# Linear attention on one Trainium2 core: Q's features stored as pairs of rows and transposed as 4-byte elements, and half a block of V's masks moved from VectorE to ScalarE

## The chip, the cores and the metric

The kernel runs on 1 core of one Trainium2 chip. The metric is the device time of one execution in microseconds (us), smaller being better. Its engines are named as in the profile: PE (TensorE's matmuls), PEld (its weight loads), DVE (VectorE), ACT (ScalarE), POOL (GpSimd) and SP (SyncE). POOL and SP also issue DMA transfers, and the core's 16 DMA engines carry them.

## What is computed

Q, K and V are float32 of shape 8 x 12 x 512 x 64: 96 heads of 512 rows with 64 features. For each head:

```
Q_feat = max(0, Q) + 1
K_feat = max(0, K) + 1
KV = K_feat^T V                      (64 x 64)
K_sum = sum of K_feat over the rows  (64)
out = (Q_feat KV) / (Q_feat . K_sum + 1e-10)
```

There is no softmax and nothing of size 512 x 512. Every input is read once and every output written once: 37.75 MB read from HBM and 12.58 MB written.

## The kernel before

**Layout.** The rows of all heads form one long list. 4096 rows (8 heads, "an eight") lie in SBUF as 128 partitions of 32 consecutive rows, so a head occupies 16 partitions. Two eights form a stage, and there are 6 stages (s = 0 to 5). Each stage is worked as two groups, g = 2s and 2s + 1 (12 groups). For K and V a group is half of the stage's rows; for Q it is half of the 8 rows `c` of each of 4 runs `r` in a partition, for both eights `n`.

**Loads and stores.** `load_pair(s)` (L129) has POOL issue three transfers for a stage, V, K and Q in this order, each turning float32 into bfloat16 on the way (2 MB read, 1 MB written). Only stage 0 is cut into smaller loads; its first half of Q comes as float32 through SP. Raw inputs have two buffers each (`IN_BUFS`), so the loads of stage s + 2 wait until the raw tiles of stage s are used up. The loop at L359 issues `load_pair(s + 2)` behind iteration s. Stores of groups 0 to 5 are issued by POOL only behind the last load, one store per group (L363); groups 6 to 9 follow by POOL, and the last two groups are stored by SP in several pieces (L142 to L151).

**The work on a group.** DVE makes K's features (`k_features`, L158) and Q's (`q_features`, L175) by one instruction of two scalar operations for each eight. For the matmul that forms KV, V must be laid out so that four heads can share one accumulation: `v_blocks` (L165) writes V four times, block `b` multiplied by a column of ones and zeros (`mask[:, b]`) that keeps only the partitions of head `b`. DVE writes blocks 0 and 1 and the first half (eight n = 0) of block 2; ACT writes the other half of block 2 and block 3. `keys_values` (L182) runs 64 matmuls for a group on these; ACT copies the finished KV of a stage out of PSUM (`keys_values_copies`, L203). A column of V's layout holds the mask itself, so K_sum comes out as a 65th column.

Q must be turned so that its 64 features lie on partitions. `transposes` (L214) runs 16 TensorE transposes of 128 x 128 bfloat16 for a group: for each run `r` and each row `c` of the group's four, the two eights' 64 features side by side become 128 partitions. They fill two PSUM tiles `qt_ps` of 8 transposes each, and `transpose_copies` (L224) has ACT copy each tile (1024 elements per partition) into `qt`. There are two such PSUM tiles in all, so the next 8 transposes wait for ACT. `out_matmuls` (L229) then multiplies: 8 matmuls for each of a group's four PSUM cells, with 64 columns of `qt` as weights. `norms` (L246) has DVE take reciprocals of the denominators and multiply, which gives the output rows.

**Order.** The instructions are written out in order for each engine (`tc.manual_schedule`, `iteration`, L275). In iteration s, output of stage s - 1 is woven into the work on stage s. DVE's order is: norms of the first group of stage s - 1, the four Q features of stage s, K features and V blocks of its second group, norms of the second group of stage s - 1, then K features and V blocks of the next stage's first group. ACT's is: V blocks, four copies of `qt_ps`, V blocks, four copies of KV. In the last iteration (`end`), the K features and V blocks come first and the transposes of the second group come later.

The functions that the diff touches and their callers, with the profile's line numbers:

Of the kernel before, what the change touches and what calls it, by code (L numbers as in the profile page):

```python
# [8 lines left out]
FP32 = mybir.dt.float32  # L9
BF16 = mybir.dt.bfloat16  # L10
# [9 lines left out]
def kernel(  # L20
# [15 lines left out]
    nc = tc.nc  # L36

    B, H, S, D = Q.shape
    P = 128
    C = 8  # L40
    C2 = 2 * C
    C4 = 4 * C
    R = 4
# [15 lines left out]
    const = ctx.enter_context(tc.tile_pool(name="const", bufs=1))  # L59
    in_pool = ctx.enter_context(tc.tile_pool(name="in_pool", bufs=IN_BUFS))  # L60
    kf_pool = ctx.enter_context(tc.tile_pool(name="kf_pool", bufs=2))
    qf_pool = ctx.enter_context(tc.tile_pool(name="qf_pool", bufs=3))
    mid_pool = ctx.enter_context(tc.tile_pool(name="mid", bufs=2))
# [3 lines left out]
    psum = ctx.enter_context(tc.tile_pool(name="psum", bufs=2, space=bass.MemoryType.PSUM))  # L67
    psum_qt = ctx.enter_context(tc.tile_pool(name="psum_qt", bufs=2, space=bass.MemoryType.PSUM))

    identity = const.tile([P, P], BF16, name="identity")  # L70
    NV = 4
    v_all = const.tile([P, 2, 2, C2, 4, DV], BF16, name="v_all")

    mask_row = const.tile([P, 396], FP32, name="mask")
    mask = mask_row[:, 0:4]
    kva_all = const.tile([P, NV, 4, 2, D1], BF16, name="kva_all")
    kva_diag = [kva_all[:, i] for i in range(NV)]
# [5 lines left out]
    qfs = {}  # L83
    qts = {}
    outs = {}
    cells_of = {}
    qt_ps = {}
# [65 lines left out]
    def feature(dst, src):  # L153
        nc.vector.tensor_scalar(  # L154
            out=dst, in0=src, scalar1=1.0, scalar2=1.0, op0=ALU.add, op1=ALU.max
        )
# [8 lines left out]
    def v_blocks(g, engine):  # L165
        v_raw = raw["v", g]
        for b in range(4):
            block = v_all[:, g % 2, :, :, b, 0:D]
            cut = 2 if b < 2 else 1 if b == 2 else 0
            if engine == "dve" and cut > 0:  # L170
                nc.vector.tensor_scalar_mul(block[:, 0:cut], v_raw[:, 0:cut], mask[:, b : b + 1])  # L171
            if engine == "act" and cut < 2:
                nc.scalar.mul(out=block[:, cut:], in_=v_raw[:, cut:], mul=mask[:, b : b + 1])  # L173

    def q_features(g):  # L175
        q_raw = raw.pop(("q", g))
        qf = qf_pool.tile([P, R, C // 2, 2, D], BF16, name="qf")
        for n in range(2):
            feature(qf[:, :, :, n], q_raw[n])
        qfs[g] = qf  # L180

    def keys_values(g, lo=0, hi=C2):  # L182
# [29 lines left out]
                )  # L212

    def transposes(g):  # L214
        qf = qfs.pop(g)
        if g % 2 == 0:
            qts[g // 2] = mid_pool.tile([P, C, P, R], BF16, name="qt")
        qt_ps[g] = [psum_qt.tile([P, 2, R, P], BF16, name="qt_ps") for _ in range(2)]
        for half in range(2):
            for c in range(2):  # L220
                for r in range(R):
                    nc.tensor.transpose(qt_ps[g][half][:, c, r], qf[:, r, 2 * half + c, :, :], identity)  # L222

    def transpose_copies(g):  # L224
        for half, t in enumerate(qt_ps.pop(g)):
            lo = g % 2 * 4 + 2 * half
            nc.scalar.copy(out=qts[g // 2][:, lo : lo + 2], in_=t.rearrange("p c r q -> p c q r"))  # L227

    def out_matmuls(g, h, i):  # L229
        qt = qts[g // 2]  # L230
        kva = kva_diag[(g // 2 * 2 + h) % NV]
        o_ps = psum.tile([P, 2, BANK], FP32, tag="ps", name="o_ps")
        for c in range(4 * i, 4 * i + 4):
            for j in range(2):
                b = 2 * (g % 2) + j
                q = 16 * (4 * h + b)
                nc.tensor.matmul(  # L237
                    o_ps[64 * j : 64 * j + 64, c // 2 % 2, (c % 2) * W : (c % 2) * W + W],
                    lhsT=qt[:, c, q : q + 16, :],
                    rhs=kva[:, b],  # L240
                    start=True,
                    stop=True,
                )
        cells_of[g, h, i] = o_ps
# [18 lines left out]
    def output(g, between=()):  # L263

        cells = [(g, h, i) for h in range(2) for i in range(2)]
        for k in range(4):
            if k >= 2:
                norms(*cells[k - 2])
                if k - 2 < len(between):
                    between[k - 2]()  # L270
            out_matmuls(*cells[k])
        norms(*cells[2])
        norms(*cells[3])

    def iteration(s):  # L275
# [6 lines left out]
        def turned(g):  # L282
            transposes(g)
            transpose_copies(g)
# [12 lines left out]
        if end:  # L297
            k_features(b)
            v_blocks(b, "dve")
        v_blocks(b, "act")  # L300
        output(a - 2, [lambda lo=lo: keys_values(a, lo, lo + quarter) for lo in (0, quarter)])
        keys_values(a, 2 * quarter, C2)
        q_features(a)
        q_features(b)
        if not end:
            k_features(b)
            v_blocks(b, "dve")
# [14 lines left out]
    with tc.manual_schedule():  # L322
# [8 lines left out]
            out=mask,  # L331
            in_=identity.rearrange("p (h b x) -> p b h x", h=2, b=4),
# [3 lines left out]
        for i in range(2):  # L336
            t = v_all[:, i].rearrange("p n c b x -> p (n c) b x")
            nc.vector.memset(t[:, :, :, D1:], 0.0)
            nc.vector.tensor_copy(  # L339
                out=t[:, :, :, D], in_=mask[:, None, :].to_broadcast([P, 2 * C2, 4])  # L340
# [5 lines left out]
        blocks(0)  # L346
        keys_values(0)
        q_features(0)
        q_features(1)
        transposes(0)  # L350
        blocks(1)
        transpose_copies(0)
        transposes(1)
        transpose_copies(1)
        keys_values(1)
        load_pair(2)
# [42 lines left out]
```

## Time and profile before

| | |
|---|---|
| Time, median of 3 runs | 126.3 us (126.06 to 126.33) |
| The profiled execution: time, span of its instructions | 126.47 us, 124.7 us |
| PE busy / PEld busy | 72.2 us (58%) / 54.4 us (44%) |
| DVE busy | 81.9 us (66%), 185 instructions |
| ACT busy | 68.4 us (55%), 73 instructions |
| POOL busy | 24.8 us (20%) |
| Transposes, PE L222 | 192 of 219 ns, 13.7 us busy (they overlap) |
| Copies of `qt_ps`, ACT L227 | 24 of 1024 ns, 22.7 us |
| Q features, DVE L154 | 22 of 430 ns from bfloat16, 2 of 685 ns from float32 |
| V blocks on DVE, L171 | 24 of 759 ns (whole), 12 of 477 ns (half) |
| V blocks on ACT, L173 | 12 of 1998 ns (whole), 12 of 1158 ns (half) |
| HBM traffic over the span | 404 GB/s |

The profile is of one execution. The span runs from the first to the last instruction; the rest of the execution's time, 1.8 us here, lies around it. Busy time counts the time in which an engine ran at least one instruction, and its rows by slices or windows show when that was. The DMA share is the time that the 16 DMA engines' packets took, as a share of 16 times the stretch; overlapping packets can bring it a little above 1. GB/s counts bytes as they arrive, so a load that turns float32 into bfloat16 counts half of what it reads.

### The profile page before, as it was taken

The page shows a single profiled execution, that of the slowest core. Times are in us where ns is not written, and L with a number is a line of the kernel's source. Part 1 is how long each engine was busy: PE and PEld are TensorE (multiplying, and loading weights), DVE is VectorE, ACT ScalarE, POOL GpSimd, SP SyncE. Part 2 cuts the span into 40 slices and gives each one's busy share as a digit, 9 for nine tenths or more (in the row PEclk, how much of TensorE's full clock was granted, in tenths as well). Part 3 has the DMA queues.
Part 4 walks back from the last instruction along what each step waited for, and adds up shares of the span by engine and source line. Part 5 has one row for each costly group of instructions (what it writes and reads, how often), then busy time and mean ns, then how long its engine had stood idle before and what let it go on. Part 6 is the DMA issues. An engine that isn't in the chain of part 4 may idle for free.

```text
span 124.7 us, 3086 instructions
## 1 busy us (share of the span) xinstructions
PE 72.2 (58%) x1344; PEld 54.4 (44%) x1344; DVE 81.9 (66%) x185; ACT 68.4 (55%) x73; POOL 24.8 (20%) x52
## 2 busy tenths in 40 slices
PE   0000199692397949976796927979429995550000
PEld 0000299591266725754465714567216774320000
DVE  0475643006679997999979979798997945990000
ACT  0005827928955999199947998059990196000000
POOL 6990001500000600033000890220210202000000
PEclk9999999999859995899769995599975799955555
DMA  3999999999999999999999999999999999999991
GB/s 74 344 216 217 214 212 210 214 214 222 210 212 210 218 222 212 212 212 214 221 214 213 212 216 216 218 213 210 214 350 422 413 417 413 413 413 418 411 388 64
DMA packets 8902, 32.18 MB, mean 258 GB/s; under 512 B 568, under 2 KB 824, under 8 KB 8760
## 3 DMA queue, kind: packets, MB, share of 16 engines
q0 software_dynamic: 7520, 28.84, 93.9%
q1 hardware_dynamic: 1368, 3.15, 6.8%
q8 instruction: 10, 0.16, 0.5%
q14 instruction: 4, 0.03, 0.1%
HBM read 37.75 MB, written 12.58 MB: 404 GB/s over the span
## 4 chain that ended last, share of the span: by engine, by line
PE 32%; DMA 21%; ACT 18%; DVE 14%; issue 3%; POOL 1%; ACTq 0%; POOLq 0%
PE kva_ps L195 21%; DMA k_raw<-in_K_dram 14%; ACT qt L227 9%; PE o_ps L237 7%; DMA v_raw<-in_V_dram 7%; ACT v_all L173 6%; DVE o_sb L254 6%; DVE v_all L171 4%; PE qt_ps L222 4%; ACT kva_all L209 2%; DVE kf L154 2%; DVE recip L253 1%; ACT L173 1%; POOL v_raw L111 1%; POOL k_raw L114 1%
## 5 line engine op out<-in xcount | busy, mean ns | idle before, releaser
L195 PE MATMUL kva_ps<-v_all,kf 64*64 64x272 bf16 x768 | 41.0, 330 | 19.9 <-ACT v_all L173 18.3
L195 PEld LDWEIGHTS <-kf 64*64 64x64 bf16 x768 | 28.3, 125 | 25.7 <-DVE v_all L171 16.4
L173 ACT ACTIVATE v_all<-v_raw,mask 128x1024 bf16<-128x1024 bf16 (+1 forms) x24 | 36.5, 1578 | 3.1 <-DMA v_raw<-in_V_dram 3.0
L254 DVE TENSOR_TENSOR o_sb<-o_ps,recip 128x512 f32<-128x512 f32 x48 | 33.2, 691 | 1.7
L227 ACT COPY qt<-qt_ps 128x1024 bf16<-128x1024 bf16 x24 | 22.7, 1024 | 19.6 <-PE qt_ps L222 19.6
L237 PE MATMUL o_ps<-kva_all,qt 128*64 128x130 bf16 x384 | 21.4, 253 | 14.1 <-ACT kva_all L209 9.2
L237 PEld LDWEIGHTS <-qt 128*64 128x64 bf16 x384 | 14.9, 126 | 23.8 <-issue 9.6
L171 DVE TENSOR_SCALAR v_all<-v_raw,mask 128x2048 bf16<-128x2048 bf16 (+1 forms) x36 | 22.0, 665 | 3.2 <-DMA v_raw<-in_V_dram 3.2
L154 DVE TENSOR_SCALAR kf<-k_raw 128x1024 bf16<-128x1024 bf16 x24 | 9.4, 434 | 12.0 <-DMA k_raw<-in_K_dram 12.0
L222 PE MATMUL qt_ps<-identity,qf 128*128 128x128 bf16 x192 | 13.7, 219 | 4.9 <-ACT qt L227 4.8
L253 DVE RECIPROCAL recip<-o_ps 128x8 f32<-128x8 f32 x48 | 9.6, 201 | 8.3 <-PE o_ps L237 8.2
L111 POOL DMA_DIRECT2D v_raw<-in_V_dram x5 | 3.7, 730 | 53.5 <-ACT qt L227 23.7
L222 PEld LDWEIGHTS <-qf 128*128 128x128 bf16 x192 | 11.2, 97 | 7.0 <-issue 6.4
L138 POOL DMA_DIRECT2D out_dram<-o_sb x10 | 8.1, 819 | 25.5 <-DVE o_sb L254 13.7
L209 ACT CAST kva_all<-kva_ps 64x260 bf16<-64x260 f32 x24 | 9.0, 374 | 3.8 <-PE kva_ps L195 3.5
L154 DVE TENSOR_SCALAR qf<-q_raw 128x1024 bf16<-128x1024 bf16 x22 | 8.2, 430 | 0.1
L173 ACT ACT_TABLE_LOAD x1 | 1.3, 1283 | 10.7 <-DMA v_raw<-in_V_dram 10.7
L124 POOL DMA_DIRECT2D q_raw<-in_Q_dram x5 | 3.6, 722 | 0.0
L111 POOL DMA_DIRECT2D k_raw<-in_K_dram x5 | 3.6, 719 | 0.0
L330 DVE TENSOR_REDUCE mask<-identity 128x4 f32<-128x128 bf16 x1 | 0.3, 285 | 4.7 <-POOL identity masks.py:199 4.7
L344 POOL MEMSET kva_all<- 128x130 bf16 x16 | 2.4, 204 | 0.0
L339 DVE CAST v_all<-mask 128x128 bf16<-128x128 f32 x2 | 2.2, 1644 | 0.0
(11 smaller groups left out, 6.0 us busy)
## 6 DMA issues: line engine op xcount, KB each, us to landing
out_dram<-o_sb POOLq DMA_DIRECT2D x10, 1024.0 KB, 24.6
v_raw<-in_V_dram POOLq DMA_DIRECT2D x5, 1024.0 KB, 13.5
k_raw<-in_K_dram POOLq DMA_DIRECT2D x5, 1024.0 KB, 17.7
q_raw<-in_Q_dram POOLq DMA_DIRECT2D x5, 1024.0 KB, 21.9
o_sb<-in_Q_dram SPq DMA_DIRECT2D x1, 1024.0 KB, 5.0
k_raw<-in_K_dram POOLq DMA_DIRECT2D x2, 512.0 KB, 9.7
v_raw<-in_V_dram POOLq DMA_DIRECT2D x2, 512.0 KB, 11.6
out_dram<-o_sb SPq DMA_DIRECT2D x1, 1024.0 KB, 11.5
```

The source lines that it names most:

```text
L111: nc.gpsimd.dma_start(out=t, in_=drams[x][:, 2 * s : 2 * s + 2])
L138: nc.gpsimd.dma_start(out=o_to[:, g % 2 : 2 * NP : 2], in_=outs[s][:, g % 2 : 2 * NP : 2], single_packet=True)
L154: nc.vector.tensor_scalar(out=dst, in0=src, scalar1=1.0, scalar2=1.0, op0=ALU.add, op1=ALU.max)
L171: nc.vector.tensor_scalar_mul(block[:, 0:cut], v_raw[:, 0:cut], mask[:, b : b + 1])
L173: nc.scalar.mul(out=block[:, cut:], in_=v_raw[:, cut:], mul=mask[:, b : b + 1])
L195: nc.tensor.matmul(halves[h][64 * eight : 64 * eight + 64, 0 : 4 * DV], lhsT=kf[ps, c, n, :], rhs=v_all[ps, g % 2, n, c], start=first, sto ...
L209: nc.scalar.copy(out=kva[ps, :, n, :], in_=halves[h][ps, 0 : 4 * DV].rearrange("p (b x) -> p b x", b=4)[:, :, 0:D1],)
L222: nc.tensor.transpose(qt_ps[g][half][:, c, r], qf[:, r, 2 * half + c, :, :], identity)
L227: nc.scalar.copy(out=qts[g // 2][:, lo : lo + 2], in_=t.rearrange("p c r q -> p c q r"))
L237: nc.tensor.matmul(o_ps[64 * j : 64 * j + 64, c // 2 % 2, (c % 2) * W : (c % 2) * W + W], lhsT=qt[:, c, q : q + 16, :], rhs=kva[:, b], sta ...
L253: nc.vector.reciprocal(out=recip, in_=cells[:, :, :, :, D:D1])
L254: nc.vector.tensor_tensor(out=outs[g // 2][:, 2 * h + g % 2 : 2 * NP : NP, 4 * i : 4 * i + 4].rearrange("p n (b c) d -> p b c n d", b=2), ...
```

## The change

Three things change.

1. Q's features. The tile `qf` gets another order: the rows `c` of a group are taken in twos (`x`), and the two rows' values of one feature lie side by side, `[r, c/2, n, d, x]`. The feature instruction writes a bfloat16 at every second element, 4 bytes apart, in place of neighbouring ones.
2. Transposes. Two bfloat16 values side by side are read as one 4-byte element (`bitcast(FP32)`). A group takes 8 transposes of 128 x 128 such elements in place of 16. Identity and PSUM tiles become float32; a PSUM tile still has 2 KB per partition. ACT copies 512 elements of 4 bytes in place of 1024 of 2. In `qt` the two rows now lie side by side, so `out_matmuls` takes its 64 weight columns at every second bfloat16.
3. V's masks. The half of block 2 that DVE wrote goes to ACT: DVE writes blocks 0 and 1, ACT blocks 2 and 3 whole.

```diff
-    identity = const.tile([P, P], BF16, name="identity")
+    identity = const.tile([P, P], FP32, name="identity")
...
-    mask_row = const.tile([P, 396], FP32, name="mask")
+    mask_row = const.tile([P, 336], FP32, name="mask")
...
-            cut = 2 if b < 2 else 1 if b == 2 else 0
+            cut = 2 if b < 2 else 0
...
     def q_features(g):
         q_raw = raw.pop(("q", g))
-        qf = qf_pool.tile([P, R, C // 2, 2, D], BF16, name="qf")
+        qf = qf_pool.tile([P, R, C // 4, 2, D, 2], BF16, name="qf")
         for n in range(2):
-            feature(qf[:, :, :, n], q_raw[n])
+            feature(
+                qf[:, :, :, n].rearrange("p r c d x -> p r c x d"),
+                q_raw[n].rearrange("p r (c x) d -> p r c x d", x=2),
+            )
...
     def transposes(g):
-        qf = qfs.pop(g)
+        qf = qfs.pop(g).rearrange("p r c n d x -> p r c (n d x)").bitcast(FP32)
         if g % 2 == 0:
-            qts[g // 2] = mid_pool.tile([P, C, P, R], BF16, name="qt")
-        qt_ps[g] = [psum_qt.tile([P, 2, R, P], BF16, name="qt_ps") for _ in range(2)]
+            qts[g // 2] = mid_pool.tile([P, C // 2, P, R, 2], BF16, name="qt")
+        qt_ps[g] = [psum_qt.tile([P, R, P], FP32, name="qt_ps") for _ in range(2)]
         for half in range(2):
-            for c in range(2):
-                for r in range(R):
-                    nc.tensor.transpose(qt_ps[g][half][:, c, r], qf[:, r, 2 * half + c, :, :], identity)
+            for r in range(R):
+                nc.tensor.transpose(qt_ps[g][half][:, r], qf[:, r, half], identity)

     def transpose_copies(g):
+        to = qts[g // 2].rearrange("p c q r x -> p c (q r x)").bitcast(FP32)
         for half, t in enumerate(qt_ps.pop(g)):
-            lo = g % 2 * 4 + 2 * half
-            nc.scalar.copy(out=qts[g // 2][:, lo : lo + 2], in_=t.rearrange("p c r q -> p c q r"))
+            nc.scalar.copy(
+                out=to[:, g % 2 * 2 + half].rearrange("p (q r) -> p q r", r=R),
+                in_=t.rearrange("p r q -> p q r"),
+            )
...
-                    lhsT=qt[:, c, q : q + 16, :],
+                    lhsT=qt[:, c // 2, q : q + 16, :, c % 2],
```

## The prediction

> **What bounds the kernel now.** I read the page's slices first, then the timelines of POOL and SP (who issues transfers, and when), then busy time by windows, and only then the costs of instructions.
>
> ```profile
> DVE  0475643006679997999979979798997945990000
> ...
> DMA  3999999999999999999999999999999999999991
> GB/s 74 344 216 217 214 212 210 214 214 222 210 212 210 218 222 212 212 212 214 221 214 213 212 216 216 218 213 210 214 350 422 413 417 413 413 413 418 411 388 64
> ```
>
> Two things are to be seen. DMA reads 9 from the second slice (a slice is 3.1 us) to the last but one, with no hole. And the rate has two levels: about 214 GB/s to the 29th slice, which are loads that read twice what they write (428 GB/s from HBM), then about 415 GB/s, which are stores. DVE, the busiest engine, has zeros in between and stops four slices before the end. So the transfers set the time, unless an engine lets their queue run empty. The windows confirm it:
>
> ```profile
> 46.60:60.70 14.10, 11.11 (x230) 7.96 (x224) 12.89 (x31) 11.38 (x14) 2.14 (x3) 0.88 1.06 214
> 60.70:75.70 15.00, 10.86 (x224) 7.87 (x224) 13.12 (x31) 12.27 (x14) 5.65 (x7) 0.85 1.06 215
> ...
> 114.00:116.00 2.00, 0.00 (x0) 0.00 (x0) 0.00 (x0) 0.00 (x0) 0.00 (x0) 0.50 1.04 421
> ...
> 121.00:122.00 1.00, 0.00 (x0) 0.00 (x0) 0.00 (x0) 0.00 (x0) 0.00 (x0) 0.50 0.81 297
> 122.00:123.00 1.00, 0.00 (x0) 0.00 (x0) 0.00 (x0) 0.00 (x0) 0.00 (x0) 0.50 0.17 64
> 123.00:124.70 1.70, 0.00 (x0) 0.00 (x0) 0.00 (x0) 0.00 (x0) 0.00 (x0) 0.50 0.02 9
> ```
>
> The columns behind the length are busy time of PE, PEld, DVE, ACT and POOL, the granted clock, DMA share and GB/s. The first two rows are iterations 2 and 3. One takes 14.1 us where nothing holds it up, with DVE busy 12.9 us; DMA share is 1.06 in both. After 112 us no engine computes, and DMA still has 9 us of full work.
>
> How far ahead of the DMA engines do the issuers run? That is the margin which a slower engine would have to use up:
>
> ```profile
> 41.19 0.72 POOL L111 DMA_DIRECT2D v_raw<-in_V_dram  x1 [17.70 <-DVE recip L253]
> 55.14 0.72 POOL L111 DMA_DIRECT2D v_raw<-in_V_dram  x1 [11.80 <-ACT qt L227]
> 69.15 0.72 POOL L111 DMA_DIRECT2D v_raw<-in_V_dram  x1 [11.88 <-ACT qt L227]
> ...
> 104.16 0.75 POOL L138 DMA_DIRECT2D out_dram<-o_sb  x1 [6.18 <-DVE o_sb L254]
> ...
> 108.72 0.40 SPq L143 DMA_DIRECT2D out_dram<-o_sb  x1
> 110.40 0.38 SPq L146 DMA_DIRECT2D out_dram<-o_sb  x1
> 112.08 0.34 SPq L147 DMA_DIRECT2D out_dram<-o_sb  x1
> 112.46 4.28 SPq L150 DMA_DIRECT2D out_dram<-o_sb  x2
> ```
>
> A stage's loads write 3 x 1.049 MB at 214 GB/s: 14.7 us. DVE's wait for stage 4's K (second of three) ends at 72.9 us, so its Q, 4.9 us of transfer later, lands near 77.8 us; a transfer lands some 1.4 us after its last packet (stage 5's Q would land near 92.5, and the GB/s row turns near 91), so stage 4's packets end near 76.4 us and the earlier stages' at 61.7 and 47.0. The loads behind them were issued at 69.15, 55.14 and 41.19 us: 7.2, 6.6 and 5.8 us ahead. From issue to first packet take off about 1 us (the first load is issued at 1.27 us, and packets flow from about 2): the margins are 4.8 us or more. From 91 us on a group's store is 1.049 MB of float32, which at 415 GB/s takes 2.5 us. Nine stores keep the queue full to 91 + 9 x 2.5 = 113.5 us; the tenth was issued at 104.16, 9 us ahead. The last group's first piece is needed at 91 + 11 x 2.5 = 118.5 and was issued at 110.40, 8 us ahead; its last rows are ready at 112.05 us (end of the last multiplication).
>
> **The change, part by part.** An iteration has two groups.
>
> *Q's features, DVE.* 4 instructions per iteration. No row has a bfloat16 output with gaps. Nearest below: 430 ns, the present form. [...] I take 685: the output no longer lies two to a word, as in the row with float32 input. Per iteration +4 x 255 = +1.02 us; ends 0 and +3.15 us.
>
> [...]
>
> *V's masks.* DVE loses 2 x 477 ns = 0.95 us per iteration. ACT's half (1158 ns) becomes a whole (1998): +2 x 840 = +1.68 us.
>
> *Copies, ACT.* 4 per iteration, 1024 elements at 1024 ns. From 64x260 at 374 ns to 1024 elements is 650 ns for 764 elements, 0.85 ns each; 512 come to 374 + 252 x 0.85 = 588 ns. Ends: 512 ns (half) and 1024 (time by bytes). -4 x 436 = -1.74 us; ends -2.05 and 0.
>
> *Transposes, PE.* A tile of 8 takes 0.57 us on the chain of waits (71 ns each); now 4 per tile. No row transposes 4-byte elements. Ends: 71 ns each, 0.28 us per tile, and four times that, 1.14 us. I take 71, the nearest row: -4 x 0.28 = -1.1 us per iteration; the far end is +2.3 us.
>
> [...]
>
> *Weights of the out matmuls*, every second element: between nothing and a doubling of the 14.9 us of PEld L237, +2.5 us per iteration. I take nothing, since a load has the same 64 columns. *Identity in float32*: POOL's two instructions (259 and 290 ns) and DVE's reduction (285 ns) may at most double, below 1 us, before 8 us, where 15 us of loads are queued. Traffic and the issues of transfers stay the same.
>
> **Sum per iteration:** DVE +1.02 - 0.95 = +0.07 us, ACT -1.74 + 1.68 = -0.06, PE -1.1. DVE's wait for the transposed Q shrinks rather than grows: PE waits 0.65 and 0.31 us for copies in each iteration, and these halve. Five iterations shift the compute by some -1 to +0.5 us. What hides it is the transfers: 4.8 us ahead for loads, 8 for stores. So 0 in the end, the span 124.7 and the execution 126.5 us; the median of the three runs is 126.3, within their spread, and I predict on that. For chances, 0.2% (0.25 us) is about what a measurement can tell from no change.
>
> **Rivals.**
>
> *A, a better ragged end: faster.* After 121 us the packets are 0.81 + 0.17 + 1.7 x 0.02 = 1.0 us of full work, spread over more than 2 us. If earlier last outputs let SP's stores run sooner beside POOL's, a packed end would be at 122.0 us in place of some 123.2. At most 1.2 us, likely half: 125.7 us. For it: ACT's and PE's shares of the last chain shrink. Against it: SP's issues at 112.46 were held for 4.28 us, so its queue was full, and an earlier start there puts no bytes away sooner.
>
> [...]
>
> *C, PE becomes late (transposes at four times, or doubled weight loads).* +2.3 to 2.5 us on PE, which idles 3.0 us of iteration 2 and waits 1 us of it for the copies that get shorter. [...]
>
> *D, a worse ragged end: slower.* A few tenths of slip change which engine has the last packets: +0.3 to +0.8 us, 126.8 us.
>
> **How the numbers follow.** Forecast, with the simple form of C in it: 0.55. A 0.20, B with the double form of C 0.11, D 0.14. Faster 0.20, same 0.55, slower 0.25. The range reaches from A's middle, somewhat exceeded (125.5), over D (127.1); B lies outside with 0.11, and some of A's and D's tails. The forecast's own range is 126.05 to 126.55.
>
> **What would show it.** Right: DMA share still 1.0 and above through every window to 121 us, GB/s at the two levels; features near 685 ns, copies near 590, V blocks on ACT 1998 each; loads issued within 1 us of 41.2, 55.1 and 69.2. Wrong: a hole in the DMA row, with the load issued later than 47, 61 or 76 us; features above 1 us; a last multiplication later than 118 us; or an end that moves while the share stays full to 121 us, which would be A or D.

## The result and the profile after

The changed kernel takes 126.75 us (median of 16 runs, 126.42 to 128.88), the kernel before 126.38 us in the same session (16 runs, 126.02 to 126.55). The ratio is 1.0027, 95% interval [1.0019, 1.0036]: slower by 0.3 us. The forecast was no change. Runs more than 1.5% above a kernel's fastest, here the one of 128.88 us, are left out of the ratios and of the rests in the table below.

The page's first line and its slices, in the order in which the kernel before was read:

```profile
PE 69.6 (56%) x1248; PEld 52.4 (42%) x1248; DVE 82.5 (66%) x173; ACT 68.9 (55%) x73; POOL 27.1 (22%) x52
...
DVE  0476741009149999999999979799997965960000
...
DMA  3999999999999999999999999999999999999991
GB/s 84 340 211 210 217 214 214 215 215 214 213 214 215 211 214 219 214 213 211 215 217 215 213 214 215 215 215 213 214 360 416 418 410 414 418 413 411 413 377 57
```

DMA has no hole, and the rate has the same two levels. The busy times moved by less than 1 us on DVE and ACT. PE lost 96 matmuls (x1344 before) and 2.6 us; the 2.6 us are no sure effect of the change, since another execution of the kernel before (e1 below) has 69.8 us with all 1344. POOL gained 2.3 us in issuing the stores (819 to 1046 ns each). The timelines of POOL and SP, and DVE's last multiplication:

```profile
42.92 0.72 POOL L111 DMA_DIRECT2D v_raw<-in_V_dram  x1 [18.67 <-ACT qt L230]
...
56.13 0.72 POOL L111 DMA_DIRECT2D v_raw<-in_V_dram  x1 [11.05 <-ACT qt L230]
...
69.34 0.72 POOL L111 DMA_DIRECT2D v_raw<-in_V_dram  x1 [11.06 <-ACT qt L230]
```

```profile
110.64 0.69 DVE L260 TENSOR_TENSOR o_sb<-o_ps,recip 128x512 f32<-128x512 f32 x1
```

The loads are issued 1.7, 1.0 and 0.2 us later than before, and nothing is lost by it; the last multiplication starts 0.7 us earlier (111.36 before). Two executions of the kernel before differ as much as that: in e1's profile its last load is issued at 68.32 us (69.15 in the profile before) and its last multiplication starts at 110.86. The windows at the end:

```profile
120.00:121.00 1.00, 0.00 (x0) 0.00 (x0) 0.00 (x0) 0.00 (x0) 0.00 (x0) 0.50 1.00 380
121.00:122.00 1.00, 0.00 (x0) 0.00 (x0) 0.00 (x0) 0.00 (x0) 0.00 (x0) 0.50 0.78 286
122.00:123.00 1.00, 0.00 (x0) 0.00 (x0) 0.00 (x0) 0.00 (x0) 0.00 (x0) 0.50 0.19 70
```

DMA shares of 0.78 and 0.19 stand against 0.81 and 0.17: the end of the transfers is the same. So is the span: its mean over the runs is 124.63 us after and 124.62 us for the kernel before (its 32 runs on record beside e1). The 0.3 us appear in no window. They lie **outside the span**: each run's time less its span has the median 1.77 us before (the same 32 runs; 1.72 to 1.85 in all sessions) and 2.02 us after (1.97 to 2.73). Below, this difference is called the rest.

What in the program could change what runs outside the span? One line of the page's queues did change, the packets that fetch instructions. Before, then after:

```profile
q14 instruction: 4, 0.03, 0.1%
```

```profile
q14 instruction: 3, 0.02, 0.1%
```

The columns are packets, MB and share. These packets are 8192 bytes each; TensorE's code has a queue of its own, q8, with 10 packets of 16384 bytes in both. That q14's last one is VectorE's is read from its moving with VectorE's instructions in the runs below. In the kernel before, q14's fourth is the only one behind 112 us; the same view of the window 112 to 124.7 us:

```profile
q14 instruction: 1, 0.01, 0.2%
```

It comes at 116.7 us, 4.6 us after the last multiplication has ended, beside stores that run to 123 us. After, there is none in that stretch. DVE's instructions went from 185 to 173.

### The profile page after: what moved, and what is told of

Same layout as the page of the kernel before. It is cut to its first block, busy times and chain, and to the rows that moved or that the text cites. A ratio compares the mean times of both kernels' runs of the same rounds, so it can differ in the third digit from the quotient of the medians.

```text
span 124.8 us, 2888 instructions
## 1 busy us (share of the span) xinstructions
PE 69.6 (56%) x1248; PEld 52.4 (42%) x1248; DVE 82.5 (66%) x173; ACT 68.9 (55%) x73; POOL 27.1 (22%) x52
## 3 DMA queue, kind: packets, MB, share of 16 engines
q1 hardware_dynamic: 1368, 3.15, 6.9%
## 4 chain that ended last, share of the span: by engine, by line
DVE 32%; PE 22%; DMA 21%; ACT 10%; issue 2%; POOL 1%; ACTq 0%; POOLq 0%
DVE o_sb L260 14%; DMA k_raw<-in_K_dram 14%; PE kva_ps L198 14%; DMA v_raw<-in_V_dram 7%; DVE v_all L171 6%; ACT v_all L173 6%; DVE qf L154 5%; PE qt_ps L225 4%; PE o_ps L243 4%; DVE kf L154 3%; DVE recip L259 3%; ACT qt L230 2%; ACT kva_all L212 1%; ACT L173 1%; POOL v_raw L111 1%
## 5 line engine op out<-in xcount | busy, mean ns | idle before, releaser
L198 PE MATMUL kva_ps<-v_all,kf 64*64 64x272 bf16 x768 | 38.4, 316 | 24.5 <-ACT v_all L173 19.9
L173 ACT ACTIVATE v_all<-v_raw,mask 128x2048 bf16<-128x2048 bf16 x24 | 46.6, 1994 | 2.2 <-DMA v_raw<-in_V_dram 2.1
L198 PEld LDWEIGHTS <-kf 64*64 64x64 bf16 x768 | 27.4, 119 | 29.6 <-DVE v_all L171 15.5
L243 PE MATMUL o_ps<-kva_all,qt 128*64 128x130 bf16 x384 | 20.7, 247 | 12.9 <-ACT kva_all L212 6.8
L230 ACT COPY qt<-qt_ps 128x512 f32<-128x512 f32 x24 | 12.9, 588 | 18.1 <-PE qt_ps L225 18.1
L171 DVE TENSOR_SCALAR v_all<-v_raw,mask 128x2048 bf16<-128x2048 bf16 x24 | 17.3, 764 | 3.1 <-DMA v_raw<-in_V_dram 3.1
L225 PE MATMUL qt_ps<-identity,qf 128*128 128x128 f32 x96 | 13.6, 286 | 3.4 <-DVE qf L154 2.1
L138 POOL DMA_DIRECT2D out_dram<-o_sb x10 | 10.4, 1046 | 22.3 <-DVE o_sb L260 7.2
L154 DVE TENSOR_SCALAR qf<-q_raw 128x1024 bf16<-128x1024 bf16 x22 | 14.6, 737 | 0.4 <-DMA q_raw<-in_Q_dram 0.4
L225 PEld LDWEIGHTS qt_ps<-identity,qf 128*128 128x128 f32 x96 | 10.5, 144 | 6.0 <-DVE qf L154 2.6
```

Source lines behind the costliest of these rows:

```text
L138: nc.gpsimd.dma_start(out=o_to[:, g % 2 : 2 * NP : 2], in_=outs[s][:, g % 2 : 2 * NP : 2], single_packet=True)
L154: nc.vector.tensor_scalar(out=dst, in0=src, scalar1=1.0, scalar2=1.0, op0=ALU.add, op1=ALU.max)
L198: nc.tensor.matmul(halves[h][64 * eight : 64 * eight + 64, 0 : 4 * DV], lhsT=kf[ps, c, n, :], rhs=v_all[ps, g % 2, n, c], start=first, sto ...
L225: nc.tensor.transpose(qt_ps[g][half][:, r], qf[:, r, half], identity)
L230: nc.scalar.copy(out=to[:, g % 2 * 2 + half].rearrange("p (q r) -> p q r", r=R), in_=t.rearrange("p r q -> p q r"),)
L243: nc.tensor.matmul(o_ps[64 * j : 64 * j + 64, c // 2 % 2, (c % 2) * W : (c % 2) * W + W], lhsT=qt[:, c // 2, q : q + 16, :, c % 2], rhs=kv ...
```

## The experiments

All times are medians; the ratio is to the kernel before on the same chip. "Rows" are DVE's records in the trace, its waits and drains included (194 before, 182 after). The fetch column has the last 8192-byte packet from 108 us on, also behind the span where the trace has it. Another such packet comes at 101.8 to 106.0 us in every run, with 79 to 84 of ACT's rows begun, however many DVE has; it is left out.

| Run | DVE rows | Last 8192-byte fetch, span of that profile | Rest, us | Ratio [95%] |
|---|---|---|---|---|
| before | 194 | 116.7, 124.7 | 1.77 | |
| after | 182 | none, 124.8 | 2.02 | 1.0027 [1.0019, 1.0036] |
| e1 before again | 194 | 116.2, 124.5 | 1.75 | 1.0002 [0.9994, 1.0011] |
| e2 masks only | 182 | none, 124.5 | 2.03 | 1.0032 [1.0020, 1.0044] |
| e3 Q only | 194 | 116.0, 124.6 | 1.81 | 1.0009 [1.0001, 1.0018] |
| e4 features only | 194 | 116.7, 124.4 | 1.80 | 1.0000 [0.9992, 1.0009] |
| e5 after, 12 more | 193 | 127.1, 126.8 | 1.75 | 1.0143 [1.0130, 1.0156] |
| e6 after, 1 long | 183 | none, 124.8 | 2.12 | 1.0034 [1.0019, 1.0049] |
| e7 after, 6 more | 187 | 128.0, 126.2 | 2.13 | 1.0193 [1.0180, 1.0206] |
| e8 before, 116 more | 309 | none, 128.5 | 1.79 | 1.0254 [1.0234, 1.0274] |
| e9 after, 13 wide | 194 | 115.4, 124.7 | 1.82 | 1.0008 [1.0000, 1.0017] |
| e10 after, 2 fewer | 180 | none, 124.6 | 1.79 | 1.0010 [0.9998, 1.0022] |
| e11 after, 6 wide | 187 | 126.7, 124.9 | 2.06 | 1.0035 [1.0021, 1.0049] |
| e12 before, K joined | 182 | none, 124.6 | 2.03 | 1.0020 [1.0011, 1.0028] |
| e13 before, 32 bytes | 195 | 110.8, 126.5 | 1.78 | 1.0154 [1.0140, 1.0169] |
| e14 Q only, twice | 194 | 119.2, 124.7 | 1.78 | 1.0001 [0.9992, 1.0009] |
| e15 after, 2 fewer, twice | 180 | none, 127.5 | 1.77 | 1.0093 [1.0058, 1.0128] |
| e16 after, 2 fewer, 96 early | 180 | none, 124.7 | 1.79 | 1.0007 [0.9998, 1.0016] |
| e17 after, 96 early | 182 | none, 124.6 | 2.01 | 1.0033 [1.0020, 1.0046] |

### Which part brings it: e1 to e4

**e1**, the kernel before without an edit, shows what the comparison can tell.

> The kernel before, unchanged, measured as the others are, so that its spans are known over many runs. All theories: ratio 1.000 within 0.001. Theory T (the end of the stores: the changed kernel's last outputs come 0.7 us sooner, SP's stores then run longer beside POOL's and the last packets fall worse): spans near 124.3, 0.3 below the changed kernel's median of 124.6, and the rest of the time (time less span) 2.0 us as in the changed kernel. Theory O (the loss lies outside the span, in the start or the end of the execution): spans 124.6 as in the changed kernel, the rest 1.7 to 1.8 us.

**e2**, V's masks alone:

```diff
-            cut = 2 if b < 2 else 1 if b == 2 else 0
+            cut = 2 if b < 2 else 0
```

> Of the change only the half block that goes from VectorE to ScalarE. VectorE loses 0.95 us per iteration, ScalarE gains 1.7. Theory T: the last outputs move by less than 1 us, and the time follows them: 1.000 to 1.003. [...]

**e3**, the change with that line put back:

```diff
-            cut = 2 if b < 2 else 0
+            cut = 2 if b < 2 else 1 if b == 2 else 0
```

> Of the change only Q's features, transposes and copies; the masks are divided as before. [...] Theory T: follows the moment of the last outputs, which I expect within 1 us of before: 0.999 to 1.003.

**e4**, only the new order of Q's features, with bfloat16 transposes of every second element as before in number:

```diff
-        qf = qf_pool.tile([P, R, C // 2, 2, D], BF16, name="qf")
+        qf = qf_pool.tile([P, R, C // 4, 2, D, 2], BF16, name="qf")
...
-                    nc.tensor.transpose(qt_ps[g][half][:, c, r], qf[:, r, 2 * half + c, :, :], identity)
+                    nc.tensor.transpose(qt_ps[g][half][:, c, r], qf[:, r, half, :, c], identity)
```

> Only the new order of Q's features, written 4 bytes apart; 16 bfloat16 transposes per group read every second element, copies and masks as before. VectorE gets about 1.2 us more per iteration and nothing back. [...] Theory T: the last outputs come later than before, by some 1 to 3 us, so SP's stores start later: the time falls or rises by up to 0.3 us with them (a fall would speak for T most clearly). The prediction's margins: no more than that, since the loads are 4.8 us ahead.

e1 has the mean span 124.65 us and the rest 1.75: the loss lies outside the span (theory O), and theory T's shorter spans of the kernel before are not there. The features take 737 ns in e4 and 738 in e3 as in the whole change, and cost 1.0000 and 1.0009, so their longer instructions are not the 0.3%. The masks alone cost what the whole change costs, e2's 1.0032. They make the compute later, not earlier: e2's last multiplication starts at 113.28 us and its load issue moves from 69.15 to 72.61 us.

```profile
113.28 0.69 DVE L254 TENSOR_TENSOR o_sb<-o_ps,recip 128x512 f32<-128x512 f32 x1
```

```profile
72.61 0.71 POOL L111 DMA_DIRECT2D v_raw<-in_V_dram  x1 [12.77 <-ACT qt L227]
```

But e2's mean span, 124.73 us, exceeds that of the kernel before by only 0.1 us, and most of the loss is again rest (2.03). The whole change has no such lateness and has the same rest. So lateness is not what costs. The two kernels share ACT's longer masks and 12 DVE instructions fewer; e2 can't tell these apart, e12 below can.

### Is it the number of DVE instructions? e5 to e8

The theory, C in the expectations: DVE's code comes in the packets of 8192 bytes, and where the last block boundary falls decides whether its fetch is hidden under the stores (116.7 us in the kernel before) or stands in what runs behind the span. How many instructions a block holds is an estimate from TensorE's code: between its first and its tenth packet of 16384 bytes PE and PEld have 1162 and 1157 instructions in the kernel before (26.9 to 105.3 us) and 1106 and 1104 in the kernel after (27.9 to 112.9 us), 258 and 246 to a packet. That would be 129 and 123 to one of 8192 bytes; the expectations take 128. The edits add memsets of a scratch tile that nobody reads. They stand in the start, behind the copies of the first `qt_ps` tiles in the program's order, so DVE does them ahead of iteration 1.

```diff
+    scratch = const.tile([P, 1], FP32, name="scratch")
...
+        for _ in range(12):
+            nc.vector.memset(scratch, 0.0)
```

**e5** is this on the kernel after. **e6** has one memset of 768 elements, the time of several but one instruction. **e7** has 6. **e8** has 116, on the kernel before.

> The changed kernel with 12 one-element memsets of a scratch tile on VectorE, while it waits for stage 1's K; VectorE's program is then as long as before the change. The runs so far: the span is the same in all kernels (median 124.6 to 124.7 us), and the rest of the time, time less span, is 1.77 us before, 2.02 in the changed kernel, 2.03 with the masks alone, 1.80 with the features alone. Theory C (the number of VectorE's instructions: its code comes in blocks of 128 instructions, 8192 bytes; before the change a block is fetched some 4.6 us behind its last multiplication, under the stores; with 12 instructions fewer that fetch is missing in the span and its block is fetched behind it): the fetch near 116 us is back, the rest is 1.75 to 1.80 us, the ratio 1.000 (within 0.001). Theory T (where the last outputs fall): no change from the changed kernel, rest 2.02, ratio 1.002 to 1.003. Theory S (ScalarE's longer instructions): the same as T.

> The control for the 12: the changed kernel with one memset of 768 elements (about 0.9 us) in the same place, as much of VectorE's time in a single instruction. Theory C: rest 2.0 us, ratio 1.0025, no fetch near 116 us. If time spent there were what counts, it would come out as with the 12.

> The changed kernel with 6 of the memsets. Theory C: a step, not a slope: either 1.77 us and the fetch, or 2.02 us and none, nothing between; which one is open, since the edge lies somewhere among the 12. A cost per instruction would give 1.9 us and ratio 1.0013.

> The kernel before with 116 memsets in the same place: 12 short of a whole block of 128, so the edge lies as in the changed kernel though nothing of the change is made. VectorE has 9.2 us of waiting there; the memsets may take some 7 to 9 us, which the margins hide. Theory C: rest 2.0 us, no fetch behind the last outputs, ratio 1.002 to 1.003. Theories T and S: rest 1.77, ratio 1.000 to 1.001.

By the rest, e5 (1.75), e6 (2.12) and e7 (2.13) came as the theory has it; by the time, all but e6 missed. e5, e7 and e8 lost 1.7 to 3.2 us in the span (means), which nothing in the theory explains, and e8's rest stayed at 1.79 where 2.0 was expected. The page of e8:

```profile
DMA  3999999999999999999999999999999999999991
GB/s 127 298 208 209 214 214 214 214 217 212 217 212 217 212 147 168 209 224 205 218 212 217 212 221 209 219 210 218 217 390 422 411 398 403 377 382 386 389 302 65
```

Two things are to be seen, and DMA's digits show neither. A hole in the loads (147 and 168 GB/s at 45 to 51 us): the 116 memsets made the first load late, issued at 46.13 us. And stores at 377 to 389 GB/s in the 35th to 38th slice in place of 414, though no engine computes behind 115.4 us. The second is in e5 and e7 too, but not in e6. What e5, e7 and e8 share is the scratch tile of 4 bytes per partition: by the addresses in the built programs, it puts every later tile 32 bytes higher (the output tiles from byte 143360 to 143392), while e6's 3072 bytes put them at 146432.

### Number and place told apart: e9 to e13

The scratch tile of **e9** and **e11** takes e6's 3072 bytes; the memsets write one element.

```diff
+    scratch = const.tile([P, 768], FP32, name="scratch")
...
+        for _ in range(13):
+            nc.vector.memset(scratch[:, 0:1], 0.0)
```

> The last four kernels had two effects at once: a scratch tile of 4 bytes moved all tiles behind it by 32 bytes, and their stores ran at 383 to 395 GB/s in place of 414 (the one with a scratch tile of 3072 bytes did not). Here the changed kernel gets 13 memsets on VectorE with the scratch tile of 3072 bytes. Theory C, sharper: VectorE's trace rows are numbered from 0; before the change it stands at row 191 (the wait for the end of the stores) when the block of code is fetched, 5.2 us after its last multiplication. Here it stands at row 191 or a little beyond as well: fetch near 116 us, time less span 1.75 to 1.80 us, span 124.6 to 124.8 as always, ratio 1.000 to 1.001. Theory L (only the layout made the differences among the last four): rest 2.0 us, ratio 1.003.

> The changed kernel with 6 memsets and the scratch tile of 3072 bytes. Theory C: the next fetch falls a few rows behind the span: rest 2.1 us or more, span 124.6 to 124.8, ratio 1.003; a fetch shortly after the span's end may show in the trace. Theory L: as the changed kernel, 2.02 us, no such fetch.

**e10** goes the other way: the kernel after with two DVE instructions fewer, the same elements written.

```diff
-        for i in range(2):
-            t = v_all[:, i].rearrange("p n c b x -> p (n c) b x")
-            nc.vector.memset(t[:, :, :, D1:], 0.0)
-            nc.vector.tensor_copy(
-                out=t[:, :, :, D], in_=mask[:, None, :].to_broadcast([P, 2 * C2, 4])
-            )
+        t = v_all.rearrange("p i n c b x -> p (i n c) b x")
+        nc.vector.memset(t[:, :, :, D1:], 0.0)
+        nc.vector.tensor_copy(
+            out=t[:, :, :, D], in_=mask[:, None, :].to_broadcast([P, 4 * C2, 4])
+        )
```

> The changed kernel with two VectorE instructions fewer: the two memsets and two copies that fill the mask columns of V's layout once become one each over both buffers. The kernel before with 116 memsets had its next fetch 10 rows behind its last row and lost nothing outside the span (1.79 us); the changed kernel has it 9 behind (2.02 us), and with one long memset 8 (2.12). Theory C: here it is 11 behind, past what runs after the span, so no fetch at all: rest 1.78 us, ratio 1.000. A theory in which fewer instructions always cost: rest 2.0 or more, ratio 1.003.

**e12** is the kernel before with K's features of both eights in one instruction: 12 DVE instructions fewer and 1.7 us less DVE work, and nothing of the change.

```diff
-        for n in range(2):
-            feature(kf[:, :, n], k_raw[:, n])
+        feature(kf.rearrange("p c n d -> p n c d"), k_raw)
```

> The kernel before, with nothing of the change, but K's features of a group by one instruction of 2048 elements in place of two of 1024: 12 VectorE instructions fewer, as in the changed kernel, and about 1 us less of VectorE's time in all. Theory C: slower by the same 0.25 us although it does less: rest 2.0 us, span 124.6, ratio 1.002 to 1.003, no fetch near 116 us. Theories T (last outputs) and S (ScalarE's longer instructions): 1.000 or a little below.

**e13** is the kernel before with the 4-byte scratch tile and one memset.

> The kernel before with a scratch tile of 4 bytes, written once by one tiny memset on VectorE, ahead of the input tiles, so that all tiles behind it start 32 bytes later; before, the output tiles start at a multiple of 4096 bytes. This tells the layout from the memsets in the runs with 6, 12 and 116 of them. Theory A (alignment of the store's source): loads at 214 GB/s as always, stores at 383 to 395 GB/s in place of 414, span about 126.5, ratio 1.013 to 1.016. Theory M (the many memsets did it): 1.000.

e12 decides. A kernel with less to do, the same span (124.65 us in the mean) and nothing of the change is slower by 0.2%, all of it rest (2.03). Its DVE count and its queue:

```profile
PE 69.5 (56%) x1344; PEld 52.5 (42%) x1344; DVE 80.2 (64%) x173; ACT 68.4 (55%) x73; POOL 25.3 (20%) x52
...
q14 instruction: 3, 0.02, 0.0%
```

e9, with the instructions put back as memsets and ACT's longer masks kept, has the rest at 1.82 and its last block at 115.4 us, with four packets of q14 on its page again. One row decides where that block falls: e5, with 193 rows to e9's 194, fetches it at 127.1 us, behind DVE's wait for the last stores.

In e11 the fetch itself is seen where it costs. The view of the transfers from 124.9 us, where e11's last instruction ends, to 128 us:

```profile
DMA packets 1, 0.01 MB, mean 3 GB/s; under 512 B 0, under 2 KB 0, under 8 KB 0
...
q14 instruction: 1, 0.01, 0.9%
```

A single packet of code, at 126.7 us, behind the span, and a rest of 2.06. e7, with 187 rows too, has one 1.8 us behind its span as well. In the kernels with 182 or 183 rows the trace shows no packet there; that theirs is the same fetch some rows later, after the trace ends, is inferred from the row counts.

All counts agree with one boundary. With 187, 183 and 182 rows the rest is 2.01 to 2.13; with 193, 194 and 195 it is 1.75 to 1.82, the fetch being in the span in all but e5 (there it comes 0.3 us behind the span; why e5's rest is none the longer stays open); with 180 it is 1.77 to 1.79, the boundary then being so far behind that it is not reached. With the 128 rows to a block that the expectations take, e8's 309 rows stand to the next boundary as 181 stand to this one. Its rest of 1.79 fits if 181 does not reach the boundary, as 180 does not; no run has 181. That reading of e8 came after its result, and e10 is the run that put it to the test. The block at 116.7 us, fetched beside the stores, cost nothing that shows: the rest is 1.77, as with 180 rows and no such fetch. With 182 to 187 rows it is 0.24 to 0.36 us more. That at the end there is no work left to hide a fetch is the likely reason, argued and not shown.

e13 settles the other thing. One memset and 32 bytes cost 1.0154, in the span. The window of e13 from 110 to 120 us:

```profile
110.00:120.00 10.00, 1.17 (x16) 0.68 (x16) 2.27 (x5) 0.00 (x0) 0.00 (x0) 0.50 1.02 387
```

It has 387 GB/s where the kernel before has 415 in the same window, at about the same DMA share (1.03). So each packet takes longer, and no queue runs dry: behind 112 us a packet of 4096 bytes takes 171 ns in the trace (median), 159 ns in the kernel before and in e9, so 8% more. The memset itself is not the cause, since e9 has 13 of them and 414 GB/s. The loads keep 214 GB/s. The addresses 143360 and 146432 are both multiples of 1024, and 143392 is one of 32 and of no higher power of two, so these runs don't tell at which step the loss begins.

### What is left of Q's part: e14 to e17

e3, e9 and e10 keep a remainder of about 0.001, and single runs have a rest 0.2 to 1.1 us above their median in kernels with 96 transposes fewer (the kernel after, e3, e6, e7, e9, e10, e11), and in no other; e5, with four runs, has none. e10's profile is of such a run, with a rest of 2.19 us, and has TensorE's last block of 16384 bytes at 125.6 us, behind its span. The view of its transfers from 124.6 to 128 us:

```profile
q8 instruction: 1, 0.02, 2.6%
```

The theory is the same edge in TensorE's program. **e14** is e3 with every transpose issued twice into the same place, so that the program is as long as before; **e15** is e10 with the same line.

```diff
-                nc.tensor.transpose(qt_ps[g][half][:, r], qf[:, r, half], identity)
+                for _ in range(2):
+                    nc.tensor.transpose(qt_ps[g][half][:, r], qf[:, r, half], identity)
```

> Of the change only Q's part, as in e3_q_only, and each transpose is issued twice, the second writing the same values again: 96 more transposes with their weight loads bring the length of TensorE's program back to that of before. With Q's part alone the time less span was 1.73 to 2.15 us with single runs far off, against 1.72 to 1.85 before; TensorE's code comes in blocks of 16384 bytes, and in some profiles of the kernels with the shorter program the last block is fetched near 113 us, in some not at all, in one at 125.6 us, behind the span. Theory C for TensorE as well: here the last block is fetched near 105 us as before, the rest is 1.72 to 1.85 us in all runs, ratio 1.000 (within 0.0008). If Q's part costs by what its engines do: 1.001 or more, since TensorE does yet more.

> The whole change, with both edges of code moved away: two VectorE instructions fewer as in e10_after_2_fewer, each transpose twice as in e14_q_only_twice. Theory C: ratio 1.000 (within 0.0008), rest 1.72 to 1.85 us in all runs, spans 124.5 to 124.8: nothing of the change itself costs or gains. Otherwise 1.001 to 1.003.

e14 came out at 1.0001, with every run's rest between 1.75 and 1.85. e15's rest was as expected (1.74 to 1.85 in its six runs), its time was not: spans of 124.9 to 128.3 us, 127.5 in the profile. The doubled transposes, on top of ACT's longer masks, made the loads late:

```profile
59.75 0.72 POOL L111 DMA_DIRECT2D v_raw<-in_V_dram  x1 [13.25 <-ACT qt L231]
...
74.82 0.72 POOL L111 DMA_DIRECT2D v_raw<-in_V_dram  x1 [12.92 <-ACT qt L231]
```

```profile
50.00:60.00 10.00, 9.68 (x156) 7.50 (x160) 8.76 (x19) 6.48 (x8) 0.25 (x1) 0.83 1.06 214
60.00:70.00 10.00, 7.81 (x184) 5.56 (x174) 8.25 (x20) 9.47 (x9) 1.90 (x3) 0.83 1.04 198
70.00:80.00 10.00, 7.12 (x130) 5.95 (x126) 9.81 (x20) 6.84 (x9) 5.18 (x7) 1.00 1.03 187
```

The second and third stretch lack 16/214 and 27/214 of 10 us, 0.7 and 1.3 us of transfer. So the extra matmuls have to stand where no path runs. **e16** is e10 with 96 transposes of 32 x 32, read by nobody, ahead of TensorE's first useful matmul (15.8 us); **e17** is the kernel after with these alone.

```diff
+        t = psum_qt.tile([P, R, P], FP32, name="qt_ps")
+        for _ in range(96):
+            nc.tensor.transpose(t[0:32, 0, 0:32], identity[0:32, 0:32], identity[0:32, 0:32])
```

> The whole change, with the two mask-column memsets and the two copies each merged into one (VectorE 2 instructions fewer, which took the median rest around the span from 2.02 to 1.79 us but left single runs at 2.2 to 2.5), and 96 transposes of 32x32 that nobody reads ahead of TensorE's first useful matmul at 15.9 us, where TensorE is idle, so that its program is as long as before without work on any path. Theory (the end of the code of both engines is the whole loss): span 124.6, rest 1.75 to 1.85 us in every run, time ratio 0.999 to 1.001. Rival (something else of the change costs a tenth or two): ratio 1.001 to 1.003.

> The whole change with the 96 early transposes alone: TensorE's program as long as before, VectorE's still 12 instructions shorter. Theory (VectorE's code edge is the loss, TensorE's only adds single late runs): rest 2.0 us, ratio 1.002 to 1.003. Rival (TensorE's shorter program is the loss): rest 1.8 us, ratio 1.000.

```profile
4.73 5.30 PE L344 MATMUL qt_ps<-identity 32*32 32x32 f32 x96 [4.73 <-POOL identity masks.py:199]
15.82 5.22 PE L198 MATMUL kva_ps<-v_all,kf 64*64 64x272 bf16 x64 [5.79 <-ACT v_all L173]
```

The 96 are done at 10.0 us, and the first useful matmul starts at 15.82 (15.85 in the kernel after). e16 holds the whole change with both edges moved: every run's rest is 1.74 to 1.83 us, the ratio 1.0007 [0.9998, 1.0016], a remainder that can't be told from 0. e17, with TensorE's edge alone moved, keeps the rest at 2.01, but without the late single runs (1.97 to 2.06). So the length of VectorE's program is the 0.25 us, and that of TensorE's the spread. No kernel that was run is faster than the kernel before.

## Why the prediction was wrong

**The step that failed** is the last of the sum: "So 0 in the end, the span 124.7 and the execution 126.5 us". The span did come out at 124.7. The 1.8 us around it were carried over from one profile as fixed, and they grew by 0.25 us (1.77 to 2.02). The runs showed that they follow the number of VectorE's instructions, which the masks' move cuts by 12: e12 has the 0.25 us without the change, and e9, e10 and e16 have the change without them. The prediction did not ask what 12 instructions fewer would do, and no rival named it. Rival D gave nearly the measured time, 126.8 us, and that by another mechanism, so its number is luck: the ragged end is the same to 0.03 in DMA share.

By its own steps:

*What bounds it: right.* DMA full to 121 us, two levels of rate, no load late.

*Q's features: near what was taken, the size somewhat more.*

```profile
L173 ACT ACTIVATE v_all<-v_raw,mask 128x2048 bf16<-128x2048 bf16 x24 | 46.6, 1994 | 2.2 <-DMA v_raw<-in_V_dram 2.1
...
L230 ACT COPY qt<-qt_ps 128x512 f32<-128x512 f32 x24 | 12.9, 588 | 18.1 <-PE qt_ps L225 18.1
...
L154 DVE TENSOR_SCALAR qf<-q_raw 128x1024 bf16<-128x1024 bf16 x22 | 14.6, 737 | 0.4 <-DMA q_raw<-in_Q_dram 0.4
```

The row has 737 ns where 685, the row with float32 input, was taken. No run shows the far end of +3.15 us per iteration, or what it was worked out from; the runs showed +1.2 us. The two instructions from float32 rose too, from 685 to 744 ns, so with that input the gaps in the output alone cost some 60 ns, about what 737 lies above 685. In sequence four take 2.61 us (the timeline at 95.86 us), 1.42 before: +1.2 us per iteration where +1.02 was worked out.

*Masks and copies: right.* 1994 ns (1998 taken) and 588 ns (588 taken).

*Transposes: the wrong size.* Before, 16 take 1.07 us in the timeline; after, 8 take 1.09:

```profile
51.86 1.07 PE L222 MATMUL qt_ps<-identity,qf 128*128 128x128 bf16 x16
```

```profile
52.43 1.09 PE L225 MATMUL qt_ps<-identity,qf 128*128 128x128 f32 x8 [0.72 <-DVE qf L154]
...
81.50 1.09 PE L225 MATMUL qt_ps<-identity,qf 128*128 128x128 f32 x8
```

Both stand at a granted clock of 1.00. That is 136 ns each, nearly twice the 71 taken and half of the far end, whose factor of four was the author's assumption and stands in no run. A tile of 4 takes 0.55 us, as long as 8 of bfloat16 did (0.57), so the -1.1 us on PE did not exist in the transposes. The missing 1.1 us cost nothing, since PE is not late. PE's waits for copies did shrink, from 0.65 and 0.31 us in an iteration to 0.26, but a wait for the longer features that the sum does not have came in their place (0.72 us above).

*Weights at every second element: right.* A load takes 122 ns in the mean (126 before; 122 also in e13, which has the old order).

*The shift of the compute: within -1 to +0.5,* -0.7 us at the last multiplication, and only -0.2 against e1's execution of the kernel before. The terms it was made of were not right: PE's -1.1 us did not exist, and DVE's +0.07 was some +0.25. So that the range held is in part luck. The loads' issues were to stay within 1 us, and the first came 1.7 us later.

*The margins: too wide, and this run did not need them.* The prediction counted on 4.8 us from a comparison of issue times with ends of packets, less 1 us. By that reckoning e15's loads were still in time by 61.7 - 1 - 59.75 = 0.95 us and 76.4 - 1 - 74.82 = 0.6 us, and lost 0.7 and 1.3 us; e8's first was late by 46.13 + 1 - 47.0 = 0.1 us and lost 1.6 (179 GB/s in 40 to 50 us). All are 1.5 to 1.9 us off. By these the least margin of the kernel before was about 3 us in place of 4.8 (an estimate); e2's issues, up to 3.5 us later than before (72.61), cost at most 0.1 us of span.

## What to carry to other kernels

Compare time less span before comparing spans: where the span stands still, the cause is not in the windows, and an edit can cost or save by its mere number of instructions (here 12 fewer on VectorE cost 0.25 us). When a difference of a few tenths of a percent appears, run a control that alters only the instruction count, in either direction, before crediting the edit. With a control that needs a new tile, see first that the transfers keep their rate: 3072 bytes left the stores at 414 GB/s here, and 32 brought them to 387, so that such a run measures the address.

## What the runs showed of the hardware

- Code comes by DMA, in packets of 8192 bytes on one queue (q14) and of 16384 on TensorE's (q8). A block of VectorE's fetched under the stores cost nothing (rest 1.75 to 1.82 us with 194 and 195 rows, 1.77 to 1.79 with 180 and no such fetch). With 182 to 187 rows the rest was 2.01 to 2.13 us; with 187 a fetch is seen 1.8 us behind the span, with 182 and 183 it is inferred. One 0.3 us behind the span (e5, rest 1.75) cost nothing.
- Stores from tiles 32 bytes higher in SBUF ran at 387 GB/s in place of 415, 1.9 us in the span (e13, 126.6 us). At 3072 bytes higher they kept their rate (e9, 414 GB/s). Other steps were not tried.
- A 4-byte transpose of 128 x 128 took 136 ns, one of bfloat16 67 to 71 ns.
- A bfloat16 output with every second element left out took VectorE 737 ns in place of 430 for 1024 elements from bfloat16, and 744 in place of 685 from float32.
